# Where tiles begin in SBUF: pads that set the distance between a matmul's two operands

## The chip, the cores and the metric

The kernel runs on one core of one Trainium2 chip. The time is device microseconds of one execution; the kernel before was run three times, and the number to compare with is the median of these runs. Engines are named as the profile names them: PE (matmuls), PEld (the weight loads of the matmuls), DVE, ACT, POOL, and SP, from whose queue every transfer is issued.

## The reference

One layer of a hybrid block over 256 latent tokens and 256 context tokens of width 1024, all in float32. Its parts, in order:

```
x   = x   + 0.5*g1x * swiglu(modulate(rmsnorm(x)),   w13_ffn1, w2_ffn1)     # the same for ctx
q, k, v, g, f, ga, gf = split(modulate(rmsnorm(x)) @ w_in)                  # 4 heads, dk 256, dv 512
o   = bidirectional chunkwise retention over context and latents (decays per head, 2-D rope on q, k)
r   = (silu(g) * groupnorm(o)) @ p_ret
fo  = real(fft2(f, over tokens and within 4 groups of 256 channels)) @ p_four
x   = x + g2x * (sigmoid(ga)*r + sigmoid(gf)*fo) @ w_out
x   = x + 0.5*g3x * swiglu(modulate(rmsnorm(x)), w13_ffn2, w2_ffn2)
out = rmsnorm(x)
```

The shifts, scales and gates (`sh`, `sc`, `g1x` and so on) come from `silu(c) @ w_ada + b_ada`. Only the latent stream is returned.

## The kernel before, in words

**Products.** Activations lie with channels on partitions and tokens along the free axis. Every float32 product is made of three matmuls in a faster format (float32r): each operand is split in a high and a low part (`wh`, `wl` of the weights; `h..h`, `h..l` and so on of the activations), and `mm3` (lines 86 to 90) adds low x high (L88), high x low (L89) and high x high (L90) in one PSUM accumulator. So every product shows as three groups, L88, L89 and L90, under the accumulator's name. Each matmul has two operands in SBUF. The *stationary* one, 128 x 128, is brought into the array by its own weight load (PEld); the *moving* one, 256, 258 or 512 columns, is then streamed through. In the profile a row `u<-pt,ht` names the accumulator, then both operands.

**Weights.** A weight tile of 128 x 1024 is brought in by `load_w` (L70): a transfer from SP's queue into `wr`, the high part `wh` on ACT (L78), the low part `wl` on DVE (L79). Each of the three has four buffers. They lie in a pool that is opened first and never moves.

**Stages.** First the feed-forward block over both streams at once (accumulators `acc`, `pa`, `pb`, `y`, 512 columns; the last two blocks of `y` are done by stream, 256 columns). Then the mixer, head by head: `kc`, `kx`, `q` (projections), `s` (scores), `u` (probabilities by tokens), `o` (by the value weights), with `ov` (a float32 product for the group norm, not split) and `ht` (transposes of the activations, 128 columns, only at the start); the Fourier branch `f` (512 columns), `sq`, `mx` runs in between, and the gate projections `g`. Then `gg` and `ro` for each of eight blocks, and `yo` (output projection). Last the second feed-forward block over the latents alone: up `fa`, `fb` (258 columns: 256 tokens and two more for the shift), down `z`; a norm sum `ssum` is made on POOL for it, and PE reads it once (`st`, L974).

**Order and memory.** The order of instructions on each engine is set at build time by a scheduler that simulates the program. Tiles are placed at build time too: pools are stacked from the left and from the right end of a partition's memory, and a tile begins where the one before it ends. No tile is aligned to more than 32 bytes. Pools that the change touches: `ttp` (L584, later also the `mg` tiles), `ap` (L586, keys, queries, sums `ut`, probabilities `pt`, transposed tokens `ht`), `fp` and `mxp` (L762 and L775, the Fourier tiles, `mx`, `gt`), `g2` (L933, `hx` and the products of the last block). The functions are `load_w`, `w2_chunks` (L437), `ffn1_down` (L465) and `fourier_open` (L760).

**Where operands lie.** The distance used below is the byte at which a moving tile begins less the byte at which the stationary one begins, modulo 512. All slices that are used as operands step by 512 or 1024 bytes, so each product has one distance:

| products (matmuls) | columns | moving, stationary | before | in the changed kernel |
|---|---|---|---|---|
| `pa`, `pb`, `acc`, `y` (1518) | 512 | 32, 288 | 256 | the same |
| `f` (96) | 512 | 288, 480 | 320 | the same |
| `kc`, `kx`, `q`, `o`, `g`, `gg`, `ro` (2304) | 256 | 480, 288 | 192 | the same |
| `y` of the last two blocks (132) | 256 | 32, 288 | 256 | 192 |
| `s` (96), `u` (384), `sq` (48), `mx` (48) | 256 | 480, 480 | 0 | 192 |
| `yo` (192), `z` (528) | 256 | 32, 288 | 256 | 192 |
| `fa`, `fb` (1056) | 258 | 32 more for each of 16 tiles, 288 | all multiples of 32, from 256 on | 160 or 416 (high tiles), 32 or 288 (low tiles) |

Of the kernel before, what the change touches and what calls it, by code (L numbers as in the profile page):

```python
# [26 lines left out]
OUT = (P, KT, T)  # L27
UB = 4
HOOK = 0
TC_KW = dict(schedule_with_timeline_sim=True)  # L30


# [5 lines left out]
def block_kernel(ctx: ExitStack, tc: tile.TileContext, i: dict, out: bass.AP):  # L38
    nc = tc.nc
    V, S, G, PE = nc.vector, nc.scalar, nc.gpsimd, nc.tensor  # L40
# [9 lines left out]
    def fpool(stack, name, side):  # L50
        return stack.enter_context(tc.tile_pool(name=name, bufs=1, reuse_waits="tile", side=side))
# [4 lines left out]
    ada_stack = ExitStack()  # L56
    adp = fpool(ada_stack, "adp", "left")

    def bank(name):
        return psum.tile([P, 512], F32, name=name, tag="ps")  # L60

    def f32(ap):
        return ap.bitcast(F32)

    uid = [0]

    def wtile(t, name):
        return wp.tile([P, 1024], F32 if t == "wr" else F32R, name=name, tag=t, bufs=4)

    def load_w(src, n, lo_engine=None):  # L70

        uid[0] += 1
        raw, hi, lo = [wtile(t, f"{t}{uid[0]}") for t in ("wr", "wh", "wl")]
        dst = raw[:, :n]
        if len(src.shape) == 3:
            dst = dst.rearrange("p (k c) -> p k c", k=src.shape[1])
        nc.sync.dma_start(dst, src)
        S.copy(hi[:, :n], raw[:, :n])  # L78
        (lo_engine or V).tensor_tensor(lo[:, :n], raw[:, :n], f32(hi[:, :n]), op=ALU.subtract)  # L79
        return hi, lo  # L80

    def split(dst_hi, dst_lo, src):
        S.copy(dst_hi, src)
        V.tensor_tensor(dst_lo, src, f32(dst_hi), op=ALU.subtract)

    def mm3(o, w, a, start, stop):

        PE.matmul(o, w[1], a[0], start=start, stop=False)  # L88
        PE.matmul(o, w[0], a[1], start=False, stop=False)  # L89
        PE.matmul(o, w[0], a[0], start=False, stop=stop)  # L90

    def sl(pair, *idx):
        return pair[0][idx], pair[1][idx]
# [51 lines left out]
    for q in range(4):  # L145
        t = per.tile([P, 2, 512], F32, name=f"xs{q}")
# [27 lines left out]
    for q in range(4):  # L174
        cb_ps.append(bank(f"cb{q}"))
# [243 lines left out]
    def some_ada(n):  # L419
        for _ in range(min(n, len(todo))):  # L420
            ada(*todo.pop(0))
# [15 lines left out]
    def w2_chunks(src, kts):  # L437
        ws, k0 = [], 0
        for n in kts:
            w = load_w(src[:, k0 * P : (k0 + n) * P], n * P)  # L440
# [6 lines left out]
    def add_sq(ap, cols, first, name):  # L447

        sq = tp.tile([P, 512], F32, name=f"sq{name}", tag="t2k", bufs=T2K)
        w = cols.stop - cols.start  # L450
        if first:
            S.activation(ssum[0][:, cols], ap, AF.Square)
            return
        S.activation(sq[:, :w], ap, AF.Square)  # L454
        G.tensor_tensor(ssum[0][:, cols], ssum[0][:, cols], sq[:, :w], op=ALU.add)  # L455

    def y_evac(ps, j, streams, st, col0):
        for n, s in enumerate(streams):
            c = slice(s * T, (s + 1) * T)
            V.scalar_tensor_tensor(  # L460
                xs[j][:, c], ps[:, col0 + n * T : col0 + (n + 1) * T], gate_col(st, s, j),
                xs[j][:, c], op0=ALU.mult, op1=ALU.add,
            )

    def ffn1_down(hf, gs, n_ada=0):  # L465
        late = []
        if hf:
            ssum[0] = per.tile([P, 512], F32, name="ssum2", tag="ssum")
        for j in range(KT):
            some_ada(n_ada)  # L470
            ws = w2_chunks(i["w2a"][hf, j], (6, 5))
            if hf and j >= KT - 2:
                late.append((j, ws))
                continue
            ps = bank(f"y{hf}_{j}")
            for k in range(HALF):
                mm3(ps, ws[k], gs[k], k == 0, k == HALF - 1)
            y_evac(ps, j, (0, 1), 0, 0)
            if hf:
                add_sq(xs[j], slice(0, 512), j == 0, f"2_{j}")  # L480
        for s in (0, 1):
            for j, ws in late:
                ps = bank(f"y{hf}_{j}_{s}")
                c = slice(s * T, (s + 1) * T)
                for k in range(HALF):
                    mm3(ps[:, :T], ws[k], sl(gs[k], slice(None), c), k == 0, k == HALF - 1)
                    if (s, j, k) == (1, KT - 2, 3):
                        norms.append(stage2_norm(0))
                y_evac(ps, j, (s,), 0, 0)
                sq = tp.tile([P, T], F32, name=f"sq2_{j}_{s}", tag="t1k", bufs=2)  # L490
                S.activation(sq, xs[j][:, c], AF.Square)
                late_sq[s].append(sq)
# [63 lines left out]
    def decays(hd):  # L556
# [16 lines left out]
    raw = tp.tile([P, P], F32, name="unit_2", tag="t1k", bufs=2)  # L573
# [10 lines left out]
    ]  # L584

    ttp = fpool(ctx, "ttp", "left")  # L586
    tt = [ttp.tile([P, 512], F32, name=f"tt{n}", tag=f"tt{n}") for n in range(2 * HEADS)]
    ap = fpool(heads, "ap", "right")
    rope = ap.tile([P, 2, T], F32, name="rope")
    nc.sync.dma_start(rope, i["rope"])  # L590
    cos2, sin2 = [rope[:, n, :].unsqueeze(1).to_broadcast([P, 2, T]) for n in range(2)]
    keys, query, sums, probs = [
        [[ap.tile([P, 512], F32R, name=f"{nm}{n}_{x}") for x in range(2)] for n in range(cnt)]
        for nm, cnt in (("kt", 2), ("qt", 1), ("ut", UB), ("pt", 2))
    ]

    ht = [[ap.tile([P, D], F32R, name=f"ht{t}_{x}") for x in range(2)] for t in range(4)]

    def two(a):
        return a.rearrange("p (a t) -> p a t", a=2)  # L600
# [9 lines left out]
    def transposed(s, k, banks):  # L610

        for t in range(2):
            for x in range(2):
                if k % 4 == 0:
                    banks[t, x] = bank(f"ht{s}_{t}_{x}_{k}")
                c = slice((k % 4) * P, (k % 4 + 1) * P)
                PE.transpose(
                    banks[t, x][:, c].bitcast(F32R), (hc2, hx2)[s][k][x][:, t * P : (t + 1) * P], unit
                )
        if k % 4 == 3:  # L620
            c = slice((k // 4) * 512, (k // 4 + 1) * 512)
            for t in range(2):
                S.copy(ht[2 * s + t][0][:, c], banks[t, 0])
                S.copy(ht[2 * s + t][1][:, c], banks[t, 1])

    def first_unit(s, w, a, pss, hook=None):

        banks = {}
        for k in range(KT):
# [3 lines left out]
            transposed(s, k, banks)  # L633
            if hook and k == HOOK:
                hook()
# [122 lines left out]
    fs, fu, cu, mx = {}, [], [], []  # L758

    def fourier_open():  # L760
        heads.close()
        fs["fp"] = fp = fpool(mix, "fp", "right")  # L762
        dft = [fp.tile([P, 768], F32R, name=f"dft{n}") for n in range(2)]
        for n in range(2):
            raw = tp.tile([P, 512], F32, name=f"dftr{n}", tag="t2k", bufs=T2K)
            c = slice(n * 384, (n + 1) * 384)
            nc.sync.dma_start(raw[:, :384], i["dft"][:, c])
            split(dft[0][:, c], dft[1][:, c], raw[:, :384])
        fs["dft"] = dft
        for n in range(2):  # L770
            fu.append([[fp.tile([P, 512], F32R, name=f"fu{n}_{e}_{x}") for x in range(2)] for e in range(2)])
        fs["cu"] = [
            [fp.tile([P, 512], F32R, name=f"cu{n}_{x}") for x in range(2)] for n in range(4)
        ]
        mxp = fpool(mix, "mxp", "right")  # L775
        for tiles, nm, cnt in ((mx, "mx", 4), (gt, "gt", KT)):
            for n in range(cnt):
                tiles.append([mxp.tile([P, 512], F32R, name=f"{nm}{n}_{x}") for x in range(2)])
# [50 lines left out]
    gt = []  # L829
# [67 lines left out]
    for j in range(KT):  # L897
        ws = [load_w(i["wgate"][j, c], 1024) for c in range(2)]
# [6 lines left out]
        wr = [load_w(i["pret"][j, c], 1024) for c in range(2)]  # L905
# [93 lines left out]
    for j in range(KT):  # L999
        ws = w2_chunks(i["w2b"][j], (8, 8, 6))  # L1000
# [124 lines left out]
```

## Time and profile before

| | us |
|---|---|
| median of 3 runs | 1013.61 (1013.13 to 1014.77) |
| profiled execution, its own time | 1015.47 |
| its span, first to last instruction | 1013.7 |
| PE busy in the span | 984.4 (97%) |
| DVE, ACT, POOL busy | 663.9, 469.4, 62.4 |
| TensorE clock granted, mean | 0.994 |

The page gives busy times of one profiled execution, the chain of waits that ended last, and the costliest groups of instructions. A group's row gives its count, its busy time and the mean duration of one in ns. Matmuls overlap in their pipeline: one of 0.28 us may start 0.12 us behind the one before it, so a duration is not the time that a matmul costs; the spacing of their starts is. The mixer begins at 400 us of the span, the `o` of the last head end at 606, the gates `gg` and `ro` run from 670 to 783, the last block's `fa`, `fb` from 806 to 939, and `z` to 1003.

### The profile page before, as it was taken

Reading aid. Unit: us, or ns where it says so; the run is one execution under the profiler, and the core shown is the slowest. Engines: PE = TensorE matmul, PEld = TensorE weight load, DVE = VectorE, ACT = ScalarE, POOL = GpSimd, SP = SyncE. Lnnn points to the kernel's source line nnn. Section 1 sums busy time; section 2 is a strip of 40 time slices with the busy share of each in tenths; the row PEclk is TensorE's granted clock in tenths of the full one; section 3 lists DMA queues with packets and bytes.
Section 4 is the critical chain, followed back from the end, with each engine's and each line's share of the span. In section 5 each row is a group of like instructions: output and inputs, shape, how many; then the busy total and the mean of one; then the engine's idle time right before and its main releaser. Section 6 shows DMA issues by size and latency. Waiting matters only on the chain.

```text
span 1013.7 us, 16779 instructions
## 1 busy us (share of the span) xinstructions
PE 984.4 (97%) x6792; PEld 907.9 (90%) x6792; DVE 663.9 (65%) x1084; ACT 469.4 (46%) x725; POOL 62.4 (6%) x39
## 2 busy tenths in 40 slices
PE   6999999999999998999999998999999989999996
PEld 4778888888888888999999997999999989999995
DVE  7879999998334335866575538865555766676543
ACT  4454322125222423756575456754444545555541
POOL 0000000000000013000000026000000300000011
PEclk9999999999999999999999999999999999999999
DMA  8647766994322233223133434456566446656651
GB/s 337 231 176 249 235 199 212 349 402 160 104 83 75 84 112 115 64 84 125 43 126 108 158 100 150 125 185 183 181 200 187 153 161 186 185 172 182 185 174 42
DMA packets 49238, 166.84 MB, mean 165 GB/s; under 512 B 5380, under 2 KB 7044, under 8 KB 49160
## 3 DMA queue, kind: packets, MB, share of 16 engines
q1 hardware_dynamic: 49160, 165.77, 50.8%
q8 instruction: 53, 0.87, 0.3%
q14 instruction: 25, 0.20, 0.1%
HBM read 164.70 MB, written 1.05 MB: 164 GB/s over the span
## 4 chain that ended last, share of the span: by engine, by line
PE 91%; DVE 4%; ACT 2%; DMA 1%; issue 1%; POOL 0%; DVEq 0%; SPq 0%; ACTq 0%; POOLq 0%
PE y L88 4%; PE y L89 4%; PE y L90 4%; PE pa L89 3%; PE pb L89 3%; PE pa L88 3%; PE pb L88 3%; PE pb L90 3%; PE pa L90 3%; PE ro L89 2%; PE ro L90 2%; PE ro L88 2%; PE fa L89 2%; PE z L90 2%; PE z L89 2%; PE z L88 2%
## 5 line engine op out<-in xcount | busy, mean ns | idle before, releaser
L79 DVE TENSOR_TENSOR wl<-wr,wh 128x1024 fp32r<-128x1024 f32 (+1 forms) x214 | 248.8, 1164 | 202.0 <-ACT wh L78 201.2
L78 ACT CAST wh<-wr 128x1024 fp32r<-128x1024 f32 (+1 forms) x226 | 227.0, 1006 | 273.2 <-PE y L90 79.2
L191 DVE CUSTOM_DVE_ANT_0 junk<-ada,cb,sm 128x1024 bf16<-128x1024 f32 x96 | 122.9, 1280 | 5.9 <-DMA ada<-in_ada 4.4
L89 PE MATMUL y<-gl,wh 128*128 128x512 f32 (+1 forms) x198 | 72.5, 366 | 0.0
L88 PE MATMUL y<-gh,wl 128*128 128x512 f32 (+1 forms) x198 | 72.4, 366 | 0.0
L90 PE MATMUL y<-gh,wh 128*128 128x512 f32 (+1 forms) x198 | 72.3, 365 | 0.0
L455 POOL TENSOR_TENSOR ssum<-ssum,sq 128x256 f32<-128x256 f32 (+1 forms) x18 | 24.6, 1367 | 727.3 <-ACT sq L454 714.2
L89 PE MATMUL pa<-h1l,wh 128*128 128x512 f32 x152 | 59.1, 389 | 0.0
L88 PE MATMUL pa<-h1h,wl 128*128 128x512 f32 x152 | 59.1, 389 | 0.0
L90 PE MATMUL pa<-h1h,wh 128*128 128x512 f32 x152 | 59.1, 389 | 0.0
L88 PE MATMUL pb<-h1h,wl 128*128 128x512 f32 x152 | 59.1, 389 | 0.0
L89 PE MATMUL pb<-h1l,wh 128*128 128x512 f32 x152 | 59.1, 389 | 0.0
L90 PE MATMUL pb<-h1h,wh 128*128 128x512 f32 x152 | 59.1, 389 | 0.0
L89 PE MATMUL fa<-hxl,wh 128*128 128x258 f32 x176 | 50.8, 289 | 0.0
L88 PE MATMUL fa<-hxh,wl 128*128 128x258 f32 x176 | 50.8, 289 | 0.0
L90 PE MATMUL fa<-hxh,wh 128*128 128x258 f32 x176 | 50.6, 287 | 0.0
L89 PE MATMUL fb<-hxl,wh 128*128 128x258 f32 x176 | 50.1, 284 | 0.0
L89 PE MATMUL z<-g2l,wh 128*128 128x256 f32 x176 | 50.0, 284 | 0.0
L88 PE MATMUL fb<-hxh,wl 128*128 128x258 f32 x176 | 50.0, 284 | 0.0
L90 PE MATMUL fb<-hxh,wh 128*128 128x258 f32 x176 | 49.9, 283 | 0.0
L88 PE MATMUL z<-g2h,wl 128*128 128x256 f32 x176 | 49.8, 283 | 0.0
L90 PE MATMUL z<-g2h,wh 128*128 128x256 f32 x176 | 49.8, 283 | 0.0
(310 smaller groups left out, 2908.3 us busy)
## 6 DMA issues: line engine op xcount, KB each, us to landing
ada<-in_ada SPq DMA_DIRECT2D x72, 512.0 KB, 5.1
wr<-in_w13b SPq DMA_DIRECT2D x44, 512.0 KB, 4.3
wr<-in_w13a SPq DMA_DIRECT2D x38, 512.0 KB, 4.3
wrv<-in_wv SPq DMA_DIRECT2D x16, 512.0 KB, 4.3
wr<-in_wg SPq DMA_DIRECT2D x16, 512.0 KB, 4.2
wr<-in_wgate SPq DMA_DIRECT2D x16, 512.0 KB, 4.3
wr<-in_pret SPq DMA_DIRECT2D x16, 512.0 KB, 3.8
wr<-in_w2b SPq DMA_DIRECT2D x16, 512.0 KB, 3.6
```

The costliest lines, as they stand in the source:

```text
L78: S.copy(hi[:, :n], raw[:, :n])
L79: (lo_engine or V).tensor_tensor(lo[:, :n], raw[:, :n], f32(hi[:, :n]), op=ALU.subtract)
L88: PE.matmul(o, w[1], a[0], start=start, stop=False)
L89: PE.matmul(o, w[0], a[1], start=False, stop=False)
L90: PE.matmul(o, w[0], a[0], start=False, stop=stop)
L191: V.tensor_tensor_reduce(junk, raw, cb[:, s, :], 1.0, sm[:, BIAS + n : BIAS + n + 1], ALU.mult, ALU.add, mod[:, s, n : n + 1],)
L455: G.tensor_tensor(ssum[0][:, cols], ssum[0][:, cols], sq[:, :w], op=ALU.add)
```

## The change

The change moves tiles. `shifted` puts a small tile of a given size (in units of 32 bytes) into a pool, ahead of others, and clears it with a memset on DVE, so that what follows begins later. Ten such pads are added. The `hx` tiles get 288 columns of memory for their 258, so that they begin every 1152 bytes instead of every 1056. The weights of the last two blocks of `y` begin 64 bytes into their buffer (`at=16`). The tiles' numbers, sizes and uses are otherwise the same.

```diff
+LINE = 32
...
+    def shifted(pool, name, eighths):
+
+        if eighths:
+            V.memset(pool.tile([P, 8 * eighths], F32, name=name), 0.0)
...
-    def load_w(src, n, lo_engine=None):
+    def load_w(src, n, lo_engine=None, at=0):
...
-        raw, hi, lo = [wtile(t, f"{t}{uid[0]}") for t in ("wr", "wh", "wl")]
-        dst = raw[:, :n]
+        raw, hi, lo = [wtile(t, f"{t}{uid[0]}")[:, at : at + n] for t in ("wr", "wh", "wl")]
+        dst = raw
...
-            ws = w2_chunks(i["w2a"][hf, j], (6, 5))
-            if hf and j >= KT - 2:
+            in_two = hf and j >= KT - 2
+            ws = w2_chunks(i["w2a"][hf, j], (6, 5), 16 if in_two else 0)
+            if in_two:
...
     ttp = fpool(ctx, "ttp", "left")
+    shifted(ttp, "pad_ttp", 14)
...
-    keys, query, sums, probs = [
-        [[ap.tile([P, 512], F32R, name=f"{nm}{n}_{x}") for x in range(2)] for n in range(cnt)]
-        for nm, cnt in (("kt", 2), ("qt", 1), ("ut", UB), ("pt", 2))
-    ]
-
-    ht = [[ap.tile([P, D], F32R, name=f"ht{t}_{x}") for x in range(2)] for t in range(4)]
+    def several(pool, nm, cnt, width, after=0):
+        tiles = [[pool.tile([P, width], F32R, name=f"{nm}{n}_{x}") for x in range(2)] for n in range(cnt)]
+        shifted(pool, f"pad_{nm}", after)
+        return tiles
+
+    keys = several(ap, "kt", 2, 512, 6)
+    query = several(ap, "qt", 1, 512, 10)
+    sums = several(ap, "ut", UB, 512, 0)
+    probs = several(ap, "pt", 2, 512, 10)
+
+    ht = several(ap, "ht", 4, D, 6)
...
+        shifted(fp, "pad_dft", 10)
...
-        fs["cu"] = [
-            [fp.tile([P, 512], F32R, name=f"cu{n}_{x}") for x in range(2)] for n in range(4)
-        ]
+        shifted(fp, "pad_fu", 12)
+        fs["cu"] = several(fp, "cu", 4, 512, 10)
...
+    shifted(g2, "pad_g2", 15)
     hx = [
-        (g2.tile([P, W], F32R, name=f"hxh{k}"), g2.tile([P, W], F32R, name=f"hxl{k}"))
+        tuple(g2.tile([P, LINE * -(-W // LINE)], F32R, name=f"{nm}{k}")[:, :W] for nm in ("hxh", "hxl"))
         for k in range(KT)
     ]
+    shifted(g2, "pad_hx", 1)
```

The order of instructions, as built, differs in the ten memsets, which all stand on DVE and wait for nothing, and in two neighbouring instructions of PE that change places at the start of the mixer. No other engine's order changes. Two of the places follow. The first is DVE at the start of the mixer: `xr` and `h2cl` are steps of the modulated activations of the context, and PE waits for the first `h2cl`. Before:

```order
L321 SCALAR_TENSOR_TENSOR xr_0_2_3420<-xs_108,amul,rstd_0_3274 128x256
L321 SCALAR_TENSOR_TENSOR xr_0_3_3424<-xs_108,amul,rstd_0_3274 128x256
L460 SCALAR_TENSOR_TENSOR xs_112<-y_7_1_3300,gate,xs_112 128x256
L325 SCALAR_TENSOR_TENSOR h2cl_3343<-xr_0_0_3412,mod,h2ch_3342 128x256
L325 SCALAR_TENSOR_TENSOR h2cl_3345<-xr_0_1_3416,mod,h2ch_3344 128x256
```

And in the changed kernel, where lines are some six to twelve numbers higher:

```order
L327 SCALAR_TENSOR_TENSOR xr_0_3_3434<-xs_108,amul,rstd_0_3274 128x256
L466 SCALAR_TENSOR_TENSOR xs_112<-y_7_1_3300,gate,xs_112 128x256
L63 MEMSET pad_kt 128x48
L63 MEMSET pad_qt 128x80
L63 MEMSET pad_pt 128x80
L63 MEMSET pad_ht 128x48
L331 SCALAR_TENSOR_TENSOR h2cl_3343<-xr_0_0_3422,mod,h2ch_3342 128x256
L331 SCALAR_TENSOR_TENSOR h2cl_3345<-xr_0_1_3426,mod,h2ch_3344 128x256
```

Four memsets stand between the last update of `xs` and the first `h2cl`. The second place is DVE at the end of the gates, where `mg` is the last operand of the output projection. Changed kernel:

```order
L85 TENSOR_TENSOR wl_7897<-wr_7895,wh_7896 128x1024
L932 TENSOR_TENSOR sgg_7751<-sgg_7751,ro_7754 128x512
L63 MEMSET pad_g_7859 128x120
L63 MEMSET pad_hx 128x8
L933 TENSOR_TENSOR sgg_7751<-sgg_7751 128x256
L85 TENSOR_TENSOR wl_8002<-wr_8000,wh_8001 128x1024
L90 TENSOR_TENSOR mg_7847<-sgg_7751,mg_7847 128x256
```

Two memsets stand between the product with the gate and the sum that makes `mg`; before, these two followed each other.

More of the change, by code (lines that the diff above doesn't have):

```diff
@@ L77, in load_w @@
         nc.sync.dma_start(dst, src)
-        S.copy(hi[:, :n], raw[:, :n])
-        (lo_engine or V).tensor_tensor(lo[:, :n], raw[:, :n], f32(hi[:, :n]), op=ALU.subtract)
+        S.copy(hi, raw)
+        (lo_engine or V).tensor_tensor(lo, raw, f32(hi), op=ALU.subtract)
         return hi, lo
@@ L435, in ffn1_up, with w2_chunks @@
         return gated_unit(pa, pb, f"1_{m}")
-    def w2_chunks(src, kts):
+    def w2_chunks(src, kts, at=0):
         ws, k0 = [], 0
         for n in kts:
-            w = load_w(src[:, k0 * P : (k0 + n) * P], n * P)
+            w = load_w(src[:, k0 * P : (k0 + n) * P], n * P, at=at)
             ws += [sl(w, slice(None), slice(c * P, (c + 1) * P)) for c in range(n)]
@@ L771, in fourier_open @@
             fu.append([[fp.tile([P, 512], F32R, name=f"fu{n}_{e}_{x}") for x in range(2)] for e in range(2)])
-        fs["cu"] = [
-            [fp.tile([P, 512], F32R, name=f"cu{n}_{x}") for x in range(2)] for n in range(4)
-        ]
+        shifted(fp, "pad_fu", 12)
+        fs["cu"] = several(fp, "cu", 4, 512, 10)
         mxp = fpool(mix, "mxp", "right")
-        for tiles, nm, cnt in ((mx, "mx", 4), (gt, "gt", KT)):
-            for n in range(cnt):
-                tiles.append([mxp.tile([P, 512], F32R, name=f"{nm}{n}_{x}") for x in range(2)])
+        mx.extend(several(mxp, "mx", 4, 512, 0))
+        gt.extend(several(mxp, "gt", KT, 512, 0))
     def sum_and_difference(p0, p1, dst, name):
```

## The prediction

> **What bounds the kernel now.** I read the page first (busy shares, chain of waits), then PE stretch by stretch. The page leaves no doubt which engine sets the time:
>
> ```profile
> PE 984.4 (97%) x6792; PEld 907.9 (90%) x6792; DVE 663.9 (65%) x1084; ACT 469.4 (46%) x725; POOL 62.4 (6%) x39
> ...
> PE 91%; DVE 4%; ACT 2%; DMA 1%; issue 1%; POOL 0%; DVEq 0%; SPq 0%; ACTq 0%; POOLq 0%
> ```
>
> So the question is how far apart the matmuls start. The view of busy time by stretch counts them. A matmul is counted where any part of its 0.28 us lies inside, so the spacing is (length + 0.28 us) / count.
>
> ```profile
> 481.60:486.40 4.80, 4.80 (x45) 1.00 0.02 5
> 487.00:497.00 10.00, 10.00 (x86) 1.00 0.33 105
> 498.00:503.50 5.50, 5.50 (x49) 1.00 0.01 3
> 597.00:606.00 9.00, 9.00 (x82) 1.00 0.71 227
> 690.00:780.00 90.00, 90.00 (x767) 1.00 0.62 186
> 783.50:805.00 21.50, 21.50 (x182) 1.00 0.54 168
> 820.00:938.00 118.00, 118.00 (x972) 1.00 0.58 178
> 940.00:998.00 58.00, 58.00 (x485) 1.00 0.51 150
> ```
>
> All but the seventh are streams of 256-column matmuls at a full granted clock (the 1.00 behind the count), and yet they have three spacings: 112.9 ns in the first (keys of the context) and 113.2 in the fourth (`o` of the last head); 118.0 in the third (`q`) and 117.7 in the fifth (`gg`, `ro`); 119.5 in the second (`u`), 119.7 in the sixth (`yo`) and 120.2 in the eighth (`z`). The 258-column `fa`, `fb` (seventh) have 121.7. The views by tile show the same as durations, min/median/max, with nothing scattered:
>
> ```profile
> L89 PE MATMUL u<-pt,ht x29: 283/283/283, 486.9 to 497.0; 128*128 128x256 f32 x29
> L89 PE MATMUL z<-g2l,wh x162: 283/283/283, 939.8 to 997.8; 128*128 128x256 f32 x162
> L89 PE MATMUL gg<-h2xl,wh x96: 281/281/281, 698.1 to 774.1; 128*128 128x256 f32 x96
> L89 PE MATMUL o<-ut,whv x25: 276/276/276, 597.8 to 606.0; 128*128 128x256 f32 x25
> L88 PE MATMUL fa<-hxh,wl x160: 282/284/287, 822.6 to 936.1; 128*128 128x258 f32 x160
> L89 PE MATMUL fa<-hxl,wh x160: 283/284/286, 822.7 to 936.2; 128*128 128x258 f32 x160
> ```
>
> Duration less 163 ns is the spacing (283 - 163 = 120, 281 - 163 = 118, 276 - 163 = 113). Set beside the table of distances above: `u` (distance 0), `yo` and `z` (256) take 120; everything at 192 takes 118 or 113, never 120. So the distance matters, and 192 has two states. What chooses between them is seen at the edges:
>
> ```profile
> 480.54 0.59 PE L752 MATMUL ov<-os,ones_dv 128*128 128x256 f32 x2
> 480.78 0.47 PE L88 MATMUL kc<-h2ch,wl 128*128 128x256 f32 x1
> 481.08 0.28 PE L89 MATMUL kc<-h2cl,wh 128*128 128x256 f32 x1
> 481.20 0.28 PE L90 MATMUL kc<-h2ch,wh 128*128 128x256 f32 x1
> 481.32 0.28 PE L88 MATMUL kc<-h2ch,wl 128*128 128x256 f32 x1
> 481.44 0.28 PE L89 MATMUL kc<-h2cl,wh 128*128 128x256 f32 x1
> 481.56 0.28 PE L90 MATMUL kc<-h2ch,wh 128*128 128x256 f32 x1
> 481.67 0.28 PE L88 MATMUL kc<-h2ch,wl 128*128 128x256 f32 x1
> ```
>
> A break in the stream (here 0.30 us behind the float32 `ov`) lets it fall, after five matmuls, into 113 ns (0.11 from 481.56 on), and it stays there to 486.4. The `u` that follow at distance 0 put it at 120, and the `q` behind them (third stretch) is at 192 and yet at 118: it keeps that for as long as no break comes, in `gg` and `ro` over 100 us. Not every break helps: `q0` at 423.2 starts behind transposes (distance 0) and stays at 118.
>
> **The change, part by part.** The order on every engine stays as it is but for ten memsets on DVE and two neighbouring PE instructions that swap; the rest is addresses. Count of the 256-column products whose distance moves to 192: `y` 132, `s` 96, `u` 384, `sq` 48, `mx` 48, `yo` 192, `z` 528, together 1428; 2304 are at 192 already. I take 120.2 (eighth row), 117.7 (fifth) and 113.2 (fourth) as prices. A moved product is bounded by nothing gained (120.2) and by 113.2.
>
> The main question is whether, with no long stretch at 0 or 256 left in the mixer, a stream that has once fallen to 113.2 stays. For it: the 96 `o` and 48 `g0` at 595 to 612 cross tiles and accumulators at 113. Against it: where a product changes from one pair of tiles to another (`o` to `s`, `g` to `mx`) a single weight load still comes at distance 0. No row shows what one such load does; the value I take is that it doesn't matter, since the stream at 481 went through five uneven spacings and still fell to 113. The rival below takes the other end.
>
> Then, from 481 us (the first `ov` break) on:
> 1. `u` of heads 1 to 3 and `s` of heads 2, 3: 336 x (120.2 - 113.2) = 2.35 us.
> 2. `sq`, `mx` behind 635 us: 60 x 7.0 = 0.4 us. Those before 635 I count at nothing, because PE waits there:
>
> ```profile
> 606.00:635.00 29.00, 24.62 (x201) 23.54 (x200) 24.57 (x23) 20.98 (x36) 18.54 (x8) 1.00 0.49 148
> 790.90:813.40 22.50, 19.64 (x164) 19.43 (x162) 21.10 (x40) 14.22 (x25) 10.64 (x7) 1.00 0.59 182
> ```
>
> (Busy time by stretch, in the order PE, weight loads, DVE, ACT, POOL: PE 24.62 of 29 us, DVE as busy with 24.57.) Of PE's waits two matter below:
>
> ```profile
> PE st L974 <- POOL ssum L455: 3.0, 1, 3.0
> PE kc L89 <- DVE h2cl L325: 0.4, 1, 0.4
> ```
>
> 3. Products at 192 that stand at 117.7 and fall with it: `q` 96, `o` of heads 1, 2 192, `kx3` 48, `g3` to `g7` 240, `gg` 384, `ro` 576: 1536 x 4.5 = 6.9 us.
> 4. `yo`: the first 72 give 0.5 us. The other 120 lie beside DVE, busy for 21.10 of the 22.50 us from 790.9 on (second row), and in front of PE's own 3.0 us wait for `ssum`: nothing. Without that cover they are worth 0.8 us.
> 5. `z`: 528 x 7.0 = 3.7 us; nothing but PE is near its end there.
> 6. Before 481 us, from 120.2 to 117.7 alone: `u0`, `s0`, `s1` 144 x 2.5 = 0.35 us, and half of `y` (0.15; the other half sits ahead of the wait for `h2ch`): 0.5 us.
> 7. `fa`, `fb`: 1056 products. Their sixteen distances become two, 160 (hi tiles, two products of three) and 32 (lo tiles), counted within 256. What those two cost in a steady stream is not in the trace. Downward, 113.2 is the fastest state of a stream. Upward, the rows of one unit show distance 160 as it is today: hi at 0, then lo at 32, 96, 160, 224, of which the one at 160 (938.75) is longest:
>
> ```profile
> 937.89 0.29 PE L88 MATMUL fb<-hxh,wl 128*128 128x258 f32 x1
> 938.02 0.28 PE L89 MATMUL fb<-hxl,wh 128*128 128x258 f32 x1
> ...
> 938.38 0.28 PE L89 MATMUL fb<-hxl,wh 128*128 128x258 f32 x1
> ...
> 938.75 0.29 PE L89 MATMUL fb<-hxl,wh 128*128 128x258 f32 x1
> ...
> 939.11 0.28 PE L89 MATMUL fb<-hxl,wh 128*128 128x258 f32 x1
> ```
>
> The longest of all, 287, gives 124. As today's neighbours keep changing distance and a constant one behaves otherwise (118 against 113), I take the middle, 118.6: 3.1 ns under today's 121.7. Some 45 of them lie before the `ssum` wait and count nothing: 1010 x 3.1 = 3.1 us.
> 8. Ten memsets. The nearest row is
>
> ```profile
> L930 DVE MEMSET sh<- 128x16 f32 x1 | 0.1, 72 | 0.0
> ```
>
> None waits for anything. Four stand ahead of the first `h2cl`, for which PE waited 0.4 us (above): 4 x 0.07 = 0.3 us lost. The others have cover (DVE idles ahead of `dft`; `mg7` is needed only behind 63 `yo`); bare, they would cost 0.4 us.
>
> Sum: 2.35 + 0.4 + 6.9 + 0.5 + 3.7 + 0.5 + 3.1 - 0.3 = 17.2 us off the profiled 1015.47, 998.3. The median of the runs lies 1.9 under the profiled time, so **996.5 us**.
>
> [...]
>
> **The rivals.**
> - *The lock is lost at each crossing.* One load at distance 0 puts the stream back to 118. Then 113 holds only from a break to the next crossing: `u1`, `q2`, `o1` give 0.67 + 0.22 + 0.43 = 1.3 us, the same with head 2, `u3` 0.67; `s`, `sq`, `mx` 108 x 2.5 = 0.3, `yo` 0.2, `z` at 117.7 1.3; with terms 6 to 8 in all 8.4 us: 1005 us. For it: a stream at 118 kept 118 for 100 us.
> - *More than that.* The 258-column stream locks too. At 113.2 it gives 5.4 us more, 991; if only columns counted ((226 - 120) / 256 = 0.41 ns each, from the spacings of 512 and 256 columns, 107 ns in all) 11.7 us more, 985. Against it: no 258-column row today is under 282 (119).
> - *No lock, and 160 stays dear.* Every moved product gets 117.7: 1206 that count x 2.5 = 3.0 us; `fa`, `fb` at (2 x 123 + 121) / 3 = 122.3 lose 0.6, the memsets 0.3: 1011.5.
> [...]
> - *Slower.* `fa`, `fb` pay a second wait per matmul, as 512-column products show it today:
>
> ```profile
> L88 PE MATMUL f<-wh,h2xl x16: 397/397/400, 584.7 to 595.2; 128*128 128x512 f32 x16
> ```
>
> ```profile
> L89 PE MATMUL pa<-h1l,wh 128*128 128x512 f32 x152 | 59.1, 389 | 0.0
> ```
>
> `f` at distance 320 takes 8 ns more than `pa` at 256. On 120.2 that is 128: 6.3 x 1010 = 6.4 us lost against 3.0 gained and 0.3 of memsets: 1017. It decides from 126.4 ns on (4.7 over today's).
>
> **How the numbers follow.** Forecast (996.5) 0.50; more than that 0.10; lock lost (1005) 0.22; no lock 0.08; independent ports 0.05; slower 0.05. About 0.2%, 2 us, is what a measurement of this kernel can tell from no change. Faster: the first three and half of "no lock", 0.86; same: the other half and the ports, 0.09; slower 0.05. The range runs from 985 (the columns alone) to 1009, which leaves out "no lock", "ports" and "slower", 0.18.
>
> **What would show it.** Right: in the view by tile, `u`, `z`, `gg`, `ro` at 276 instead of 283 and 281, from the first `ov` on; `fa` and `fb` with one or two durations instead of a spread from 282 to 287, around 282; PE's wait for `ssum` about as long as now. `gg` at 281 but `u` of head 1 at 276 means the lock is lost at crossings. `u` and `z` still at 283 kills the reading by distance. `fa` over 289 (126 ns) would make the whole wrong.

## The result, and the profile after

The changed kernel takes **999.27 us** (median of four runs, 998.85 to 999.83) against 1013.84 (four runs, 1013.13 to 1014.77): ratio 0.986, 95% interval 0.9847 to 0.9872, 14.6 us less. The forecast was 996.5, its range 985 to 1009. The profiled execution took 999.83 us, 15.6 less than the profiled one of before; its span is 998.1. The sum of the prediction, made between profiled executions, was 17.2. Times and ratios here and below are of runs at a mean granted clock of 0.99; three runs, at 0.56 and 0.76, took 1206 to 1613 us and are left out.

Page of the changed kernel, busy time; line numbers of `mm3` are now 94 to 96:

```profile
PE 966.9 (97%) x6792; PEld 890.3 (89%) x6792; DVE 665.2 (67%) x1094; ACT 469.0 (47%) x725; POOL 62.1 (6%) x39
```

PE still runs through 97% of the span with as many matmuls, but is busy for 17.5 us less. The view by tile of the changed kernel (durations min/median/max, then the first and the last start) shows which:

```profile
L95 PE MATMUL u<-pt,ht x96: 276/276/281, 443.0 to 536.8; 128*128 128x256 f32 x96
L95 PE MATMUL s<-qt,kt x24: 276/281/283, 469.6 to 556.0; 128*128 128x256 f32 x24
L95 PE MATMUL kx<-h2xl,wh x32: 281/281/281, 472.3 to 519.6; 128*128 128x256 f32 x32
L94 PE MATMUL gg<-h2xh,wl x128: 276/276/276, 664.1 to 764.4; 128*128 128x256 f32 x128
L94 PE MATMUL ro<-gt,wl x128: 276/276/276, 669.5 to 769.8; 128*128 128x256 f32 x128
L94 PE MATMUL yo<-mg,wl x64: 276/278/359, 772.9 to 794.8; 128*128 128x256 f32 x64
L94 PE MATMUL fa<-hxh,wl x160: 282/282/283, 812.0 to 923.9; 128*128 128x258 f32 x160
L94 PE MATMUL z<-g2h,wl x176: 276/276/282, 927.2 to 987.1; 128*128 128x256 f32 x176
```

(The first three rows are of a stretch from 440 to 560 us, the seventh from 812 on.) `gg`, `ro`, `z` went from 281 or 283 to 276 throughout. `kx` of heads 2 and 3 and most of `s` stand at 281: the state of 113 ns was lost in front of them. `fa`, `fb` have 282 to 283. The same stretches in the view of busy time by stretch:

```profile
670.00:758.00 88.00, 88.00 (x778) 1.00 0.65 195
785.00:794.50 9.50, 9.50 (x83) 1.00 0.77 247
813.00:925.00 112.00, 112.00 (x935) 1.00 0.61 183
929.00:983.00 54.00, 54.00 (x479) 1.00 0.54 161
```

(Length + 0.28) / count gives 113.5 ns for `gg`, `ro`; 117.8 for the last `yo`; 120.1 for `fa`, `fb`, where the prediction had 118.6; 113.3 for `z`. For the kernel before, the starts come from these rows of the same view by tile, and from those in the prediction:

```profile
L88 PE MATMUL gg<-h2xh,wl x128: 281/281/281, 669.7 to 773.9; 128*128 128x256 f32 x128
L88 PE MATMUL yo<-mg,wl x64: 281/283/283, 782.8 to 805.4; 128*128 128x256 f32 x64
L88 PE MATMUL z<-g2h,wl x176: 278/283/286, 939.4 to 1002.8; 128*128 128x256 f32 x176
```

| stage, up to | start before | start after | gained in the stage | predicted, from terms |
|---|---|---|---|---|
| `kc` behind the first `ov` | 480.8 | 478.5 | 2.3 | 0.2 (6, 8) |
| first `gg` | 669.7 | 664.1 | 3.3 | 5.3 (1, 2, part of 3) |
| first `yo` | 782.8 | 772.9 | 4.3 | 4.3 (rest of 3) |
| `fa` of the third unit | 822.6 | 812.0 | 0.7 | 0.5 (4) |
| first `z` | 939.4 | 927.2 | 1.6 | 3.1 (7) |
| end of the span | 1013.7 | 998.1 | 3.4 | 3.7 (5) |

The total is near, but the rows are not all right, and the runs below show that most of the first is no work of the change.

### The profile page after: what moved, and what is told of

Its sections match the earlier page's. It is cut to its first block, busy times and chain, and to the rows that moved or that the text cites. A ratio compares the mean times of both kernels' runs of the same rounds, so it can differ in the third digit from the quotient of the medians.

```text
span 998.1 us, 16789 instructions
## 1 busy us (share of the span) xinstructions
PE 966.9 (97%) x6792; PEld 890.3 (89%) x6792; DVE 665.2 (67%) x1094; ACT 469.0 (47%) x725; POOL 62.1 (6%) x39
## 4 chain that ended last, share of the span: by engine, by line
PE 90%; DVE 4%; ACT 2%; DMA 1%; issue 1%; POOL 0%; DVEq 0%; SPq 0%; ACTq 0%; POOLq 0%
PE y L94 4%; PE y L96 4%; PE y L95 4%; PE pa L94 3%; PE pb L94 3%; PE pa L96 3%; PE pb L96 3%; PE pb L95 3%; PE pa L95 3%; PE ro L95 2%; PE ro L96 2%; PE ro L94 2%; PE fa L95 2%; PE fa L96 2%; PE fa L94 2%; PE fb L95 2%
```

## The experiments

My theory: the distance alone acts; a stream at 192 can stand at 113 or 118 ns, a break lets it fall to 113, and 118 comes from loads at distance 0. The rivals: something else in the change; the lock lost at each crossing; a state that nothing in the addresses foretells.

| run | median us | ratio to before, 95% |
|---|---|---|
| the change | 999.27 | 0.986 (0.9847 to 0.9872) |
| all pads 512 bytes | 1014.27 | 1.0002 (0.9992 to 1.0012) |
| hx as before | 999.46 | 0.9853 (0.9836 to 0.9869) |
| keys at 288 | 1000.7 | 0.9871 (0.9856 to 0.9885) |
| before, and one product ahead of `gg` | 1014.01 | 1.0004 (0.9995 to 1.0013) |
| attention tiles as before | 1005.14 | 0.9916 (0.99 to 0.9931) |
| hx at 64 | 998.46 | 0.9847 (0.9828 to 0.9866) |
| keys at 288, and three products | 998.48 | 0.985 (0.9837 to 0.9864) |
| Fourier tiles as before | 1005.27 | 0.9918 (0.9903 to 0.9932) |
| keys at 288, three products, hx at 64 | 998.57 | 0.9837 (0.9815 to 0.9859) |
| the same, and a product ahead of `z` | 999.9 | 0.9868 (0.9853 to 0.9884) |

(Before is from 1013.68 to 1013.80 in these.) Beside them there are two maps with one run each. What is read from a trace is read from one execution of each kernel.

### All of the change but the distances

```diff
-LINE = 32
+LINE = 2
...
-    shifted(ttp, "pad_ttp", 14)
+    shifted(ttp, "pad_ttp", 16)
...
-    shifted(g2, "pad_g2", 15)
+    shifted(g2, "pad_g2", 16)
```

(and so on: every pad 16 eighths, the offset of the weights of `y` 128 columns instead of 16).

> The change with all of its code, its ten memsets and its pads, but every pad is 512 bytes long (in the tile group where room is short the four memsets share one pad), so every operand lies where it lay before, counted within 512 bytes. My theory (the distance alone acts): no gain; u and z stay at 283 ns, gg and ro at 281, and the memsets cost at most 0.3 us: 1013.9 us. Rival (it is something else that the new code or the pads did, such as the order of two PE instructions, or who lies beside whom): some of the gain of 14.6 us appears, anywhere down to 999.3.

Measured: 1.0002, 0.9992 to 1.0012. View by tile of this kernel:

```profile
L95 PE MATMUL u<-pt,ht x128: 279/283/283, 442.5 to 582.1; 128*128 128x256 f32 x128
L95 PE MATMUL gg<-h2xl,wh x128: 281/281/281, 668.2 to 772.4; 128*128 128x256 f32 x128
L95 PE MATMUL z<-g2l,wh x176: 278/283/469, 936.7 to 1000.1; 128*128 128x256 f32 x176
```

The durations of before, so the distances are the cause, and the memsets cost nothing that can be measured. It also shows how far two executions at the same addresses lie apart: here the third unit's `fa` starts at 820.9, not 822.6, and `fa`, `fb` run at 120.6 ns, not 121.7:

```profile
820.00:932.00 112.00, 112.00 (x931) 1.00 0.60 183
```

(112.28 / 931 = 120.6.) So the sixteen distances, too, have two patterns, and the 121.7 from which term 7 started was the dearer one. And `kc` behind the first `ov` starts at 478.4 here, so most of the 2.3 us in the table's first row is not the change's. One part of it can be seen: `q0` and `kx1`, at the addresses of before, stand at 113 here and stood at 118 in the profiled execution of before. First before, then this kernel:

```profile
L89 PE MATMUL q<-h2xl,wh x15: 281/281/281, 423.7 to 428.7; 128*128 128x256 f32 x15
L95 PE MATMUL q<-h2xl,wh x15: 276/276/277, 421.7 to 426.5; 128*128 128x256 f32 x15
```

They stand at 113 in the two other kernels below that start from before, too. From the start of `q0` to that `kc` these three take 57.2 us, the change 56.7: some 0.4 us gained at an equal state of `q0`, where term 6 had 0.35.

### The hx tiles as before

```diff
-LINE = 32
+LINE = 2
```

> The change without its edit of the hx tiles: they are 1056 bytes apart again, so fa and fb see sixteen distances as before; z and all else stay as changed. My theory: fa and fb return from 120.1 to 121.7 ns apart, 1.6 x 1010 = 1.6 us, 1000.9 us, and z stays at 276 ns because its own distance is 192 and the step from 258 to 256 columns shakes the stream anyway. Rival (z is locked only because fa, fb lead into it evenly): z at 281, another 528 x 4.5 = 2.4 us, 1003.3 us.

Measured 999.46; the predicted loss of 1.6 us did not come. `fa`, `fb` of this kernel, then its `z`, by stretch:

```profile
816.00:925.00 109.00, 109.00 (x906) 1.00 0.60 183
930.00:980.00 50.00, 50.00 (x444) 1.00 0.59 174
```

109.28 / 906 = 120.6 and 50.28 / 444 = 113.2. The edit of hx is worth 0.5 ns a product against this pattern, 0.6 us in all, which these runs cannot tell from nothing; and `z` keeps its 113 without that edit.

### Keys at 288: no weight load at distance 0 between o and s

```diff
+    shifted(ap, "pad_rope", 10)
     keys = several(ap, "kt", 2, 512, 6)
-    query = several(ap, "qt", 1, 512, 10)
+    query = several(ap, "qt", 1, 512, 0)
```

> The change with the keys moved from 480 to 288 and the queries from 160 to 480 (same distance 192), so that the weight load of s behind o and behind kx1, and of kx behind s, come at 192 and no longer at 0 or 128; nothing else moves. My theory (a single load at distance 0 is what throws the stream from 113 to 118): s0, kc1, u0, q1, o0, kx2, s2, kx3, s3 go from 281 to 276 ns, 456 x 4.5 = 2.05 us, 997.2 us. Rival (any change of tiles and accumulators throws it, or the state is settled afresh at each start): the same groups stay at 281 and the time stays at 999.3.

Measured 1000.7. Both theory and rival failed as stated. The trace of the change has this at the crossing from `o` to `s`:

```profile
511.26 0.28 PE L96 MATMUL o<-ut,whv 128*128 128x256 f32 x1
511.37 0.28 PE L94 MATMUL s<-qt,kt 128*128 128x256 f32 x1
511.49 0.28 PE L95 MATMUL s<-qt,kt 128*128 128x256 f32 x1
511.61 0.28 PE L96 MATMUL s<-qt,kt 128*128 128x256 f32 x1
```

The last `o` starts 0.11 ahead of the first `s`, which starts 0.12 ahead of the next, and it stays so (118.0 on average over this `s`, 117.8 over the `kx` behind). With the keys moved, the crossings of heads 0 and 1 pass without a trace: `s0` to `o0`, `s1`, `kx2` stand at 113.3 and 113.4 ns (by their starts), where the change had 117.8 to 118.0 in all but `s1` and the 15 `kc` that stand between the two parts of `s0`. So with the loads at 0 in front of `s` gone, and those at 128 behind it, nothing throws the stream off 113 at these crossings; as `s` is slow from its first product on in the change, the load at 0 is what does it there, as the theory says (`s1` of the change shows that it need not keep one at 118: there `o0` arrived at 117.8, and the `s` behind the same crossing settled at 113, until `kx2` had 117.8 again). But then `ov` comes, and behind it the stream came out at 118 here, at 113 in the change, with the same distances in `kx`, `ov` and `kc`. First the change:

```profile
477.73 0.28 PE L96 MATMUL kx<-h2xh,wh 128*128 128x256 f32 x1
477.85 1.02 PE L765 MATMUL ov<-os,ones_dv 128*128 128x256 f32 x4
478.53 0.47 PE L94 MATMUL kc<-h2ch,wl 128*128 128x256 f32 x1
478.83 0.28 PE L95 MATMUL kc<-h2cl,wh 128*128 128x256 f32 x1
...
479.30 0.28 PE L96 MATMUL kc<-h2ch,wh 128*128 128x256 f32 x1
479.41 0.28 PE L94 MATMUL kc<-h2ch,wl 128*128 128x256 f32 x1
```

and with the keys at 288:

```profile
475.91 0.28 PE L96 MATMUL kx<-h2xh,wh 128*128 128x256 f32 x1
476.02 1.03 PE L766 MATMUL ov<-os,ones_dv 128*128 128x256 f32 x4
476.70 0.47 PE L94 MATMUL kc<-h2ch,wl 128*128 128x256 f32 x1
477.01 0.28 PE L95 MATMUL kc<-h2cl,wh 128*128 128x256 f32 x1
...
477.48 0.28 PE L96 MATMUL kc<-h2ch,wh 128*128 128x256 f32 x1
477.60 0.28 PE L94 MATMUL kc<-h2ch,wl 128*128 128x256 f32 x1
```

The last two rows are 0.11 apart in one, 0.12 in the other. The streams reach this `ov` at different paces (118 and 113), the four matmuls that the trace has of it last 377, 377, 378, 379 ns in the change and 379 each here, and they leave at different paces. At the second `ov` both come in at 118 (`kx3`) and still leave at 113 and 118, so the pace at the entry does not settle it alone. With the keys at 288 it went to 118 at the three `ov` ahead of `kc2`, `kc3` and `u3` (25.28 / 215 = 117.6 ns from 484 to 509 us), and what stands behind them gave back more than the crossings had gained. A break alone does not settle the state. What else does is not shown: it may be handed over through the break, or the keys' new place may act in another way, since the keys made from `kc` are written there.

### Before, with one 512-column product ahead of gg

```diff
         ps = bank(name)
+        if name == "gg0":
+            PE.matmul(ps, a[0][0][:, :P], ws[0][0][:, :512], start=True, stop=True)
```

> The kernel before, every address as it was, with one added 512-column product (tokens as weights, wgate as moving operand, distance 64 within 256, as f has it) into the accumulator of gg0, right before gg0 overwrites it. My theory (gg and ro stand at 118 ns only because of the state in which the stream reaches them; in all four traces o3 fell to 113 right behind the 512-column f): the product redraws the state, gg and ro go to 276 ns: 960 x 4.5 - 0.23 = 4.1 us less, 1009.6 us. Rival (only the addresses of the streams before and after decide, or the draw falls on 118 again): gg and ro stay at 281, 1013.9 us.

Measured 1.0004, 0.9995 to 1.0013: the theory failed. `gg` stays as it was:

```profile
L89 PE MATMUL gg<-h2xl,wh x128: 281/281/281, 668.3 to 772.5; 128*128 128x256 f32 x128
```

### Attention tiles as before, and Fourier tiles as before

Two runs that split the change: the first takes the pads of keys, queries, probabilities and `ht` away (`s`, `u` back at 0), the second those of `dft` and `fu` (`sq`, `mx` back at 0; the pad behind `cu` is 1024 bytes, so that `mx` and `gt` stay).

```diff
-    keys = several(ap, "kt", 2, 512, 6)
+    keys = several(ap, "kt", 2, 512, 0)
...
-    ht = several(ap, "ht", 4, D, 6)
+    ht = several(ap, "ht", 4, D, 0)
```

> The change without the pads of the attention tiles: s and u are at distance 0 again, all later pads stay. My theory: u of heads 1 to 3 goes from 113.3 to 120.0 ns (288 x 6.7 = 1.9 us), u0 and s by another 0.4, and q2, q3, o1, o2 behind them stay at 118 instead of 113 (288 x 4.5 = 1.3), f at 233.5 instead of 229 (0.4): 4.0 us more, 1003.3 us; gg and ro stay at 276 because sq and mx, which come later, are still at 192. Rival (the long stretches at distance 0 decide the state of all that follows): gg and ro back at 281 as well, another 4.3 us, 1007.6 us.

```diff
-        shifted(fp, "pad_dft", 10)
+        shifted(fp, "pad_dft", 0)
...
-        shifted(fp, "pad_fu", 12)
-        fs["cu"] = several(fp, "cu", 4, 512, 10)
+        shifted(fp, "pad_fu", 0)
+        fs["cu"] = several(fp, "cu", 4, 512, 32)
```

> The change without the pads of the Fourier tiles (fu, cu back at 480), so that sq and mx are at distance 0 again; the attention pads, mg, hx and g2 stay as changed. My theory (gg and ro owe their 113 ns to what stands right before them, that is to sq and mx at 192): g3 to g7, gg and ro return to 281 ns: 240 + 960 products x 4.5 = 5.4 us, and sq, mx another 0.4: 1005.1 us. Rival (g0 arrives at 113 from the attention, and the stream finds back by itself): gg and ro stay at 276, 999.7 us.

Measured 1005.14 and 1005.27. `u` and `gg` without the attention pads, then without the Fourier pads:

```profile
L95 PE MATMUL u<-pt,ht x128: 279/283/283, 445.2 to 584.8; 128*128 128x256 f32 x128
L95 PE MATMUL gg<-h2xl,wh x128: 276/276/276, 669.9 to 770.2; 128*128 128x256 f32 x128
```

```profile
L95 PE MATMUL u<-pt,ht x128: 276/276/281, 442.7 to 578.5; 128*128 128x256 f32 x128
L95 PE MATMUL gg<-h2xl,wh x128: 281/281/281, 664.4 to 768.6; 128*128 128x256 f32 x128
```

`gg` and `ro`, whose addresses are the same in both and in the kernel before, owe their 113 ns to the 96 products of `sq` and `mx` that precede them: a pad on tiles that they never read is worth 960 x 4.5 = 4.3 us there. The second run came out 0.2 from its expectation. The first came out 1.8 above; `q0` and `kx1` stood at 117.8 in it (0.4 us); the rest is not traced.

### Two maps

One constant distance for a whole unit of `fa`, `fb` or `z`, by shifting the split weights within larger tiles:

```diff
-        tuple(g2.tile([P, LINE * -(-W // LINE)], F32R, name=f"{nm}{k}")[:, :W] for nm in ("hxh", "hxl"))
+        tuple(g2.tile([P, 320], F32R, name=f"{nm}{k}")[:, :W] for nm in ("hxh", "hxl"))
...
-        ws = [load_w(i["w13b"][m, n], 1024) for n in range(2)]
+        ws = [load_w(i["w13b"][m, n], 1024, lines=up_lines[m]) for n in range(2)]
...
-        ws = w2_chunks(i["w2b"][j], (8, 8, 6))
+        ws = w2_chunks(i["w2b"][j], (8, 8, 6), lines=down_lines[j])
```

> A map, not a faster version: fa, fb and z with one constant distance for a whole unit (moving minus weights within 256): fa, fb of m = 0 to 21 at 192, 192, 160, 160, 224, 224, 96, 96, 64, 64, 32, 32, 128, 128, 0, 0, 192, 224, 160, 96, 64, 192, and z of j = 0 to 7 at 192, 160, 224, 96, 64, 32, 128, 0. All hx tiles lie 1280 bytes apart. My theory A (258 columns need one step more than 256, and no distance helps): fa and fb are 119 to 122 ns apart at every distance, 120 at 0. Rival B (it was the mixture of 160 and 32 that kept them from falling): at constant distance they fall to 114 or 115 ns at 192 and some others. [...] The time itself: within 6 us of 999.3 either way.

Spacing in ns, the mean of the starts of a unit:

| distance within 256 | 0 | 32 | 64 | 96 | 128 | 160 | 192 | 224 |
|---|---|---|---|---|---|---|---|---|
| `fa`, `fb` (258 columns) | 120.0 | 120.0 | 119.0 | 120.0 | 122.2 | 120.0 | 120 to 121 | 120.1 |
| `z` (256 columns) | 120.0 | 117.8 | 117.8 | 119.9 | 118.7 | 120.0 | 113.3 | 118.5 |

(The `z` at 192 without its first products.) Theory A holds but at 64: 258 columns nowhere fall to 113 or 115 (119.0 is their least). For 256 columns only 192 did (113.3), in this one order; 64 did not do as 192 (117.8), and 32 to 224 did not all fall (113.3 to 120.0). In this map the moving tiles of `z` lie alike and the weights are shifted; in the change the weights stayed and the moving tiles were shifted. Both show 120 at 0 (120.0 here, 120.2 before the change) and 113.3 at 192, so it is the distance that counts and not the place of one of the two. `z` at 192, `fb` at 0 and at 128, view by tile:

```profile
L102 PE MATMUL z<-g2l,zh x16: 276/276/276, 926.7 to 931.8; 128*128 128x256 f32 x16
L101 PE MATMUL fb<-hxh,zl x8: 283/283/283, 887.4 to 889.9; 128*128 128x258 f32 x8
L101 PE MATMUL fb<-hxh,zl x6: 285/285/285, 875.9 to 877.7; 128*128 128x258 f32 x6
```

The second map leaves the steady distance at 192 and puts one odd load ahead of each `gg` and `ro` of the kernel before:

```diff
-        ps = project(ws, hx2, f"gg{j}")[0][0]
+        ps = bank(f"gg{j}")
+        kick(ps, ws[0])
+        pair_of(ws, hx2, (ps, ps), (0, T))
...
+        kick(po, wr[0])
         for k in range(2 * KT):
```

> A map, not a faster version: the kernel before (gg and ro at distance 192, arriving at 118 ns), with one short product put ahead of each of gg0, ro0, gg1, ro1 and so on, sixteen in all, into an accumulator that is then overwritten. Ahead of every ro but ro2, and ro3, the weights of the added product are loaded at distance 0 (as behind o); ahead of gg0, gg1, gg7 the load behind it comes at 128 (as behind mx), of ro3 at 0, ahead of gg2 stand two float32 products (as in ov), of gg4, gg5, gg6 a load at 64, 160, 32. My theory (a stream at 192 keeps its state until one odd load; 0 throws it to 118, 128 lets it settle at 113): gg0, gg1, gg7 at 276 ns, each ro behind a 0 at 281. Rival (what follows depends on the state and the moment of arrival, not on the distance of the odd load): the same added product is followed by 276 in one place and by 281 in another. Second rival (one product never changes it): all stay at 281.

The list as it ran (ns are durations of the stream: 276 is the pace of 113, 281 that of 118; "own" means that the added product's weights came at that distance, "next" that the weights behind it did):

| ahead of | odd load | stream before | stream behind |
|---|---|---|---|
| `ro0`, `ro1`, `ro4`, `ro5` | 0, own | 281 | 281 |
| `gg3`, `ro6`, `ro7` | 0, own | 276 | 281 |
| `ro2` | 0, next | 276 | 276 |
| `ro3` | 0, next | 281 | 276 |
| `gg0`, `gg1` | 128, next | 281 | 281 |
| `gg7` | 128, next | 281 | 276 |
| `gg4` | 64, next | 276 | 281 |
| `gg5` | 160, next | 281 | 281 |
| `gg6` | 32, next | 281 | 276 |
| `gg2` | two float32 products | 281 | 276 |

Rows behind the 128 ahead of `gg0` and ahead of `gg7`, behind the 0 ahead of `ro6`, and behind the 0 ahead of `ro2`:

```profile
L89 PE MATMUL gg<-h2xl,wh x12: 281/281/281, 670.9 to 674.7; 128*128 128x256 f32 x12
L89 PE MATMUL gg<-h2xl,wh x13: 276/276/276, 771.9 to 776.0; 128*128 128x256 f32 x13
L89 PE MATMUL ro<-gt,wh x12: 281/281/281, 763.0 to 766.8; 128*128 128x256 f32 x12
L89 PE MATMUL ro<-gt,wh x11: 276/276/276, 706.9 to 710.3; 128*128 128x256 f32 x11
```

One part of the theory holds in the main: weights loaded at 0 while a stream stands at 113 left it at 118 three times of four here, and at `s0`, `s2`, `s3` of the change. The fourth is `ro2`, where the starts were some 118 ns apart behind the load but fell to 113 again after five products. A stream at 118 that met a 0 stayed there in four of five (`ro3` fell), and fell at `s1` of the change. For the rest the first rival is right: the same 128 is followed by 281 twice and by 276 once, and a 0 by both.

### Towards a faster kernel: hx at 64, and products that redraw the state

```diff
-    shifted(g2, "pad_g2", 15)
+    shifted(g2, "pad_g2", 12)
...
-        tuple(g2.tile([P, LINE * -(-W // LINE)], F32R, name=f"{nm}{k}")[:, :W] for nm in ("hxh", "hxl"))
+        tuple(g2.tile([P, 320], F32R, name=f"{nm}{k}")[:, :W] for nm in ("hxh", "hxl"))
...
-    shifted(g2, "pad_hx", 1)
+    shifted(g2, "pad_hx", 4)
```

> The change with the sixteen hx tiles 1280 bytes apart and all at distance 64 within 256, in place of 160 and 32 (g2, and so z, unmoved). From the map: 119.0 ns at 64 against 120.0 now: 1056 x 1.0 = 1.1 us less, 998.2 us. Rivals: fa and fb settle in another pattern when the whole stage is at 64 (120.5: 999.8 us); z, reached from another pattern, settles at 118 instead of 113 (2.4 us more: 1000.6 us).

Measured 998.46, four runs from 996.01 to 999.89. In the profiled one (999.89) `fa`, `fb` and `z`:

```profile
813.00:921.00 108.00, 108.00 (x913) 1.00 0.60 185
926.00:980.00 54.00, 54.00 (x461) 1.00 0.55 162
```

108.28 / 913 = 118.6, better than expected, and 54.28 / 461 = 117.7: the second rival came true, `z` was reached from another pattern and settled at 118. So distance 192 allows 113 and does not ensure it. That the runs near 996 had `z` at 113 would fit the 2.4 us, but they have no trace.

```diff
             ps = bank(f"u{hd}_{f2}")
+            if (hd, f2) == (HEADS - 1, 0):
+                PE.matmul(ps, hx2[0][0][:, :P], keys[0][0], start=True, stop=True)
...
         ps = bank(name)
+        if name in ("kc2", "kc3"):
+            PE.matmul(ps, hx2[0][0][:, :P], ws[0][0][:, :512], start=True, stop=True)
```

(on top of the keys at 288)

> The kernel with the keys at 288 and the queries at 480, plus one 512-column product (like f, distance 64) behind each ov that came out at 118 there: ahead of kc2, of kc3 and of u3, each into an accumulator that is then overwritten. My theory (a 512-column product redraws, and the draw behind it is 113 as for o3): kc2, u1, q2, o1, s2, kx3, kc3, u2, q3, o2, s3, u3 at 276 ns, some 3.4 us less than with the keys moved alone, minus 3 x 0.23: 998.0 us. Rival (the state is carried through such a product): all stay at 281, 1001.4 us.

Measured 998.48, 0.5 from what was expected. All from `kc2` to `s3` came out at 113, here `o` of heads 0 to 2:

```profile
L95 PE MATMUL o<-ut,whv x96: 276/276/276, 457.0 to 551.3; 128*128 128x256 f32 x96
```

So the same kind of product that did nothing ahead of `gg0` put the stream at 113 three times here. Both edits together, and then one more such product ahead of `z`:

> Moved keys and queries, the three added 512-column products, and hx at distance 64, together. Alone they gave 998.48 and 998.46 us. My theory: fa, fb at 118.7 ns as alone, 1056 x 1.3 = 1.4 us less than without, 997.1 us if z settles at 113 ns, and 2.4 more, 999.5 us, if at 118.

```diff
+            if not k0:
+                first_hi[0] = w[0][:, :512]
...
         py = bank(f"z{j}")
+        if j == 0:
+            PE.matmul(py, g[0][0][:, :P], first_hi[0], start=True, stop=True)
```

> The same with one more 512-column product (like f, distance 64) into the accumulator of z0 right before z0. My theory (behind such a product the stream settles at 113 more often than not): z at 276 ns, 0.23 us for the product: 997.3 us. Rival (z keeps the state in which fa, fb end): z at 281, 999.7 us.

Measured 998.57 (994.13 to 999.6) and 999.9 (999.29 to 1001.98). `z` of the one, then of the other:

```profile
927.00:980.00 53.00, 53.00 (x470) 1.00 0.56 165
```

```profile
926.00:980.00 54.00, 54.00 (x460) 1.00 0.54 161
```

113.4 ns without the added product, 118.0 with it: the rival. No version is safely faster than the change: the intervals of all of them overlap its own. Single executions reach 994, but nothing here makes them do so each time.

## Why the prediction was right, and where not

The direction, roughly the size and the base of the forecast stood: the gain comes from the distance of the two operands, and 192 has a state of 113 ns. How the stream keeps that state was forecast wrong, and that the sum came so near is in part luck: terms 1 to 3 fell 2.0 us short up to `gg` and term 7 1.5 us, while some 2 us of the 15.6 between the profiles belong to the profiled execution of before. No run shows the "independent ports" to which the forecast gives a chance of 0.05 and, with half of "no lock", the 0.09 of "same"; what the first run shows in their place is that with everything but the distances kept nothing was gained (1.0002). The spacing of these products goes with the distance: for `z` of the map 120.0 ns at 0 and 113.3 at 192, where with hx at 64 it was 117.7; by what means, no run here shows. Term by term:

- **The key assumption, that a single load at 0 doesn't matter, was wrong.** It left a stream that stood at 113 at 118 ns in three of four trials of the map and in front of `s0`, `s2` and `s3` of the change. The rival that counts crossings was right there: `s2`, `s3`, `kx3` stayed at 118, and head 0 ran at 118 from `s0` to `o0` but for 15 `kc`. It was wrong on the size: behind `mx` the stream found back to 113 each time (`g3`, `g4`, `g5`), so `gg` and `ro` got all of the predicted 4.3 us instead of none.
- **"A break lets it fall"** was the wrong reading of the edge at 481 us. With the old distances and with the new ones the stream came out of the first `ov` at 113, but with the keys at 288 it came out of that one and of the next two at 118. The argument held in the change, but not for the reason given. "Not every break helps", read from `q0` at 118, rested on one execution: at the same addresses `q0` stood at 113 in three others.
- **Terms 1 to 3 up to `gg`** were to give 5.3 us and gave 3.3. `u1` to `u3` gave 288 x 6.6 = 1.9, `q2`, `q3`, `o1`, `o2` 288 x 4.5 = 1.3, as said; `f`, not counted, fell from 233.4 to 229.2 ns (0.4 us). Then part went into a wait that I had not watched: PE's wait for DVE's `fu`, ahead of the first `sq`, was 2.3 us in this execution and 1.0 before:

```profile
PE sq L94 <- DVE fu L90: 2.3, 1, 2.3
```

  It was between 1.0 and 1.8 in the profiles of all other kernels, with old and new addresses alike, so most of the difference is scatter and not the change; 2.3 stands in this profile alone. It sat where the prediction said that gains count nothing.
- **Term 4** (`yo`) stood: from `yo4` on they were at 117.8 only, and it cost nothing, as the cover named there was in place; PE's wait for `ssum` was 3.2 us against 3.0 before.
- **Term 5** (`z`): 3.4 of 3.7 us; 113.3 ns but for its first products.
- **Terms 6 and 8**: 2.3 us were gained up to the first `ov`, against 0.2. At the old distances that `kc` starts at 480.8, 478.4, 478.8 and 480.6 in four profiles, against 478.5 in the change, so the row is mostly the spread of executions; the part behind the start of `q0` gives some 0.4 us to the change, as term 6 had it. The memsets cost nothing that the first run can tell.
- **Term 7 (`fa`, `fb`) is the one that failed in size**: 3.1 us predicted, 1.6 between the two profiles, and the run without the edit shows some 0.6 or less. Two errors: 118.6 was the middle of its bounds, 120.0 was measured (distance 64 would have given 118.6); and the 121.7 of before was one of two patterns at the same addresses, the other, 120.6, stood in three other kernels at these addresses. I had noted two states for 192 and did not ask whether the spread of sixteen distances had two as well.

So of 17.2 us 15.6 came between the profiles, and 14.6 between the medians; the 1.9 us that I took off for the profiled execution of before were not the same in the changed kernel, whose profiled run (999.83) lies 0.6 over its median.

## What to carry to other kernels

Where PE is the bound, the spacing of matmuls is worth reading to a nanosecond: in this kernel the bytes at which the moving tile and the weight tile begin bore on it (`z`: 120.2 ns before, 113.3 after), and 96 products of `sq`, `mx` at distance 0 set the pace of the hundred microseconds of `gg` and `ro` behind them (281 ns instead of 276), which never touch the tiles that were moved. So look for what precedes a slow stream, not only at the stream. And where a number comes in two states, take it from more than one execution before it enters a sum.

## What had not been expected of the hardware

- At one distance and one clock a stream of 256 columns has two lasting paces, 113.3 and 117.8 ns, and which one it takes depends on what ran ahead of it (`gg` at 281 ns behind `sq`, `mx` at 0, at 276 behind them at 192). Float32 products do not settle it: behind the first `ov` the stream stood at 113 in the change and at 118 with the keys at 288. The state behind a disturbance is the same from kernel to kernel in some places, but not in all: with `sq`, `mx` at 192 `gg` stood at 276 in the change, with hx as before, without the attention pads and with hx at 64, while `z`, behind hx at 64, was at 117.7 ns in one kernel and at 113.4 in another. What selects it stays open, beyond that a load at 0 in a stream at 113 led to 118 in three of four places of the second map; `q0` was at 117.8 in one execution and at 113.3 in three at the same addresses, and `o3`, behind `f` and a pause, was at 113.5 in the change and at 117.8 with hx at 64, which moves nothing that far ahead.
- 258 columns never went under 118.6 ns at any distance that was tried (hx at 64), 256 went to 113.3: between the best of each, the two columns more cost 5.3 ns.
- Distance 128 is the dearest for 258 columns (122.2), dearer than 0 (120.0, with 283 ns from the shortest to the longest).
- `f`, 512 columns at an unchanged distance of 64 within 256, has two paces as well: 229.2 ns where the `s` in front of it is at 192, 233.4 where that is at 0, and 233.4 too with the keys at 288.
